# Relu and row sum of a 64 MB input: 8-row tiles, a tail in places of its own, and the last row in halves

## The chip, the cores and the metric

The kernel runs on one core of a Trainium2 chip. The metric is the device time of one execution in microseconds (us); the profile's span, from the first to the last instruction, is about 2 us shorter. SyncE issues the DMAs here; ACT is ScalarE and DVE is VectorE. A DMA moves its bytes over 16 DMA engines in packets, each of which is one record of the trace.

## The reference

```python
x = np.random.randn(32, 512, 1024).astype(np.float32)   # 64 MiB
out = np.sum(np.maximum(x, 0), axis=-1)                  # (32, 512), float32
```

The input is read once, each element gets one max and one add, and 64 KB are written.

## The kernel before

The 16,384 rows are laid over 128 partitions, 128 rows each, so a partition's rows lie one after another in HBM. A tile takes T = 4 rows of each partition: 128 runs of 16 KB, 2 MB. SyncE issues the loads into four buffers; ACT sums two rows of a tile and DVE the other two, each row with one instruction that also accumulates. The last four rows come as tiles of 2, 1 and 1.

```python
    T = 4
    NBIG = R // T - 1
    NBUF = 4
    specs = [(i * T, T, [0, 1], [2, 3]) for i in range(NBIG)]
    r = NBIG * T
    specs.append((r, 2, [1], [0]))
    specs.append((r + 2, 1, [], [0]))
    specs.append((r + 3, 1, [], [0]))
    # ... cut
            for t, (r0, nr, act_rows, dve_rows) in enumerate(specs):    # SyncE
                b = t % NBUF
                if act_cnt[b] > 0:
                    sync.wait_ge(act_sems[b], act_cnt[b])
                if dve_cnt[b] > 0:
                    sync.wait_ge(dve_sems[b], dve_cnt[b])
                sync.dma_start(
                    bufs[:, b, : nr * D],
                    xv[:, r0 : r0 + nr, :],
                ).then_inc(dma_sems[b], 16)
    # ... cut
                    ins = dve.tensor_scalar(          # DVE, one row
                        tile, tile, 0.0, None, MAX, ADD,
                        accum_out=sums[:, g : g + 1],
                    )
```

## Time and profile before

| | before |
|---|---|
| time, median of 3 runs | 166.65 us (166.57 to 166.73) |
| span of the profiled run | 164.4 us |
| DVE / ACT busy | 47% / 43% |
| DMA in mid-stream, 80 to 120 us | 430 GB/s |
| last load landed, output issued | 161.04 us, 162.37 us |

First the page's row of DMA activity: the span in 40 slices, a digit being the mean busy share of the 16 DMA engines in tenths, and below it what they moved.

```profile
DMA  5999999999999999999999999999999999999980
GB/s 191 427 383 431 439 435 419 431 439 431 423 427 439 419 401 435 425 427 431 439 415 431 435 431 427 423 443 423 419 435 431 427 423 443 423 419 435 409 363 18
DMA packets 5042, 67.19 MB, mean 409 GB/s; under 512 B 560, under 2 KB 688, under 8 KB 944
```

The DMA engines are busy from the second slice to the last but two. Nothing can be gained in mid-stream by issuing loads sooner; only a cheaper way to move the same bytes counts.

The view of SyncE's waits (who waited for whom: total us, times, longest) looks alarming and is not:

```profile
SPq L70 <- DVE bufs L121: 139.3, 30, 7.7
```

SyncE waits for a free buffer nearly all the time, but two or three loads are always queued behind the one that runs: in the median a load lands 17.1 us after its issue, and the loads land 4.9 us apart. The queue's own waiting is the normal state of a kernel bound by transfers.

The chain of waits (start, duration, what) shows the pace in mid-stream and the end:

```profile
107.08 2.38 DVE bufs L121 x4
...
126.68 2.38 DVE bufs L121 x4
...
146.26 2.38 DVE bufs L121 x4
...
148.71 11.11 DMA bufs<-in_x_dram
...
159.83 1.23 DVE bufs L121 x2
...
161.06 1.22 DVE bufs L121
```

DVE starts a tile as soon as it has landed, so its starts are landings: 19.58 to 19.60 us for four tiles of 4 rows, which is 9.79 us for 8 rows. At the end the last row lands at 161.04, and DVE then takes 1.22 us for its 1024 columns before the sums can be stored. The timeline (start, duration, engine, line, operation) has both:

```profile
161.06 1.22 DVE L121 TENSOR_SCALAR_CACHE_REDUCE bufs<-bufs 128x1024 f32<-128x1024 f32 x1
...
162.37 0.34 SPq L85 DMA_DIRECT2D out_dram<-sums  x1
```

### The profile page before, as it was taken

To read this page: it belongs to the slowest core of one execution; us is meant where nothing else is said; L and a number is where in the kernel's file an instruction comes from. 1 tells how busy PE (TensorE), PEld (TensorE's weight loads), DVE (VectorE), ACT (ScalarE), POOL (GpSimd) and SP (SyncE) were. 2 spreads that over 40 slices of the span, in tenths; PEclk is the share of its full clock that TensorE was granted. 3 is DMA by queue.
4 is the path that set the end of the run, shared out by engine and by line. 5 is a ranking of instruction groups with operands and counts; after the bars stand their busy time and mean duration, and the time that the engine had idled before them with its cause. 6 is when DMAs were issued, how large, how long until landed. Compare 5 with 4: busy or idle time off the path is not lost.

```text
span 164.4 us, 354 instructions
## 1 busy us (share of the span) xinstructions
DVE 77.1 (47%) x130; ACT 70.3 (43%) x127; POOL 0.2 (0%) x4
## 2 busy tenths in 40 slices
DVE  0055433555433455433455533455533455543394
ACT  3055433455433455433455533455533355543370
POOL 0000000000000000000000000000000000000000
DMA  5999999999999999999999999999999999999980
GB/s 191 427 383 431 439 435 419 431 439 431 423 427 439 419 401 435 425 427 431 439 415 431 435 431 427 423 443 423 419 435 431 427 423 443 423 419 435 409 363 18
DMA packets 5042, 67.19 MB, mean 409 GB/s; under 512 B 560, under 2 KB 688, under 8 KB 944
## 3 DMA queue, kind: packets, MB, share of 16 engines
q1 hardware_dynamic: 5040, 67.18, 96.7%
q14 instruction: 2, 0.02, 0.0%
HBM read 67.11 MB, written 0.07 MB: 409 GB/s over the span
## 4 chain that ended last, share of the span: by engine, by line
DMA 85%; DVE 13%; issue 0%; SPq 0%; DVEq 0%
DMA bufs<-in_x_dram 85%; DVE bufs L121 13%; SPq L70 0%; DVEq L53 0%
## 5 line engine op out<-in xcount | busy, mean ns | idle before, releaser
L121 DVE TENSOR_SCALAR_CACHE_REDUCE bufs<-bufs 128x1024 f32<-128x1024 f32 x65 | 76.8, 1217 | 85.2 <-DMA bufs<-in_x_dram 85.1
L100 ACT ACTIVATE bufs<-bufs 128x1024 f32<-128x1024 f32 x63 | 66.0, 1048 | 88.7 <-DMA bufs<-in_x_dram 88.7
L100 ACT ACTIVATION_READ_ACCUMULATOR bufs<-bufs 128x1 f32 x63 | 11.7, 186 | 0.0
L121 DVE DVE_READ_ACCUMULATOR bufs<-bufs 128x1 f32 x65 | 5.4, 83 | 0.0
L100 ACT ACT_TABLE_LOAD x1 | 1.3, 1283 | 0.7 <-PEq L145 0.7
L145 POOL MEMSET const-bfloat16-1.0<- 128x1 bf16 x1 | 0.1, 101 | 0.0
L145 POOL MEMSET const-uint8-127<- 128x1 uint8 x1 | 0.1, 101 | 0.0
L145 POOL MEMSET const-float32-0.0<- 128x1 f32 x1 | 0.1, 98 | 0.2 <-issue 0.2
L145 POOL MEMSET const-float32-1.0<- 128x1 f32 x1 | 0.1, 98 | 0.0
## 6 DMA issues: line engine op xcount, KB each, us to landing
bufs<-in_x_dram SPq DMA_DIRECT2D x31, 2048.0 KB, 17.1
bufs<-in_x_dram SPq DMA_DIRECT2D x1, 1024.0 KB, 14.7
bufs<-in_x_dram SPq DMA_DIRECT2D x2, 512.0 KB, 9.3
out_dram<-sums SPq DMA_DIRECT2D x1, 64.0 KB, 1.5
```

Source lines behind the costliest of these rows:

```text
L100: ins = act.activation(tile, tile, RELU, accum_out=sums[:, g : g + 1],)
L121: ins = dve.tensor_scalar(tile, tile, 0.0, None, MAX, ADD, accum_out=sums[:, g : g + 1],)
L145: nc = _bacc.Bacc("TRN2", target_bir_lowering=False, num_devices=1)
```

## The change

It means to keep more bytes in flight with fewer DMAs, to issue the last loads without waiting, and to shorten what is left to compute when the last bytes have landed. Tiles have 8 rows (4 MB, runs of 32 KB), in three buffers. The last 8 rows come as tiles of 4, 2 and 1 rows and two halves of a row, each in a place of its own, so nothing holds back their issue. DVE sums the two halves of the last row into two columns and adds them; a wait on a semaphore stands ahead of the add.

```diff
-    T = 4
-    NBIG = R // T - 1
-    NBUF = 4
+    T = 8
+    NBUF = 3
+    H = D // 2
     ... (cut: items of 8 rows, half of them to ACT, half to DVE)
+    items.append(dict(rows=(r, 4), act=[(0, D, r), (D, D, r + 1)],
+                      dve=[(2 * D, D, r + 2), (3 * D, D, r + 3)]))
+    items.append(dict(rows=(r + 4, 2), act=[(D, D, r + 5)], dve=[(0, D, r + 4)]))
+    items.append(dict(rows=(r + 6, 1), act=[(0, D, r + 6)], dve=[]))
+    items.append(dict(half=(r + 7, 0), act=[], dve=[(0, H, r + 7)], notrack=True))
+    items.append(dict(half=(r + 7, H), act=[], dve=[(0, H, "scratch")], dve_post_add=r + 7))
+    # the last items have a place of their own: they are issued without a wait
+    OWN = [-5, -4, -3, -2, -1]
     ... (cut: buffers and semaphores for them)
+                if post is not None:
+                    dve.wait_ge(half_sem, 2)
+                    dve.tensor_tensor(
+                        sums[:, post : post + 1],
+                        sums[:, post : post + 1],
+                        scratch[:, 0:1],
+                        ADD,
+                    ).then_inc(dve_sems[b], 1)
```

More of the change, by code (lines that the diff above doesn't have):

```diff
@@ L1 @@
+from contextlib import ExitStack
 import concourse.bass as bass
@@ L28, in bass_relu_sum_kernel @@
     ADD = mybir.AluOpType.add
-    specs = [(i * T, T, [0, 1], [2, 3]) for i in range(NBIG)]
-    r = NBIG * T
-    specs.append((r, 2, [1], [0]))
-    specs.append((r + 2, 1, [], [0]))
-    specs.append((r + 3, 1, [], [0]))
-    assert sum(s[1] for s in specs) == R
+    items = []
+    nbig = (R - T) // T
+    for i in range(nbig):
+        r0 = i * T
+        act = [(j * D, D, r0 + j) for j in range(T // 2)]
+        dve = [(j * D, D, r0 + j) for j in range(T // 2, T)]
+        items.append(dict(rows=(r0, T), act=act, dve=dve))
+    r = nbig * T
+    assert R - r == T == 8
+    items.append(
+        dict(
+            rows=(r, 4),
+            act=[(0, D, r), (D, D, r + 1)],
+            dve=[(2 * D, D, r + 2), (3 * D, D, r + 3)],
+        )
+    )
+    items.append(
+        dict(rows=(r + 4, 2), act=[(D, D, r + 5)], dve=[(0, D, r + 4)])
+    )
+    items.append(dict(rows=(r + 6, 1), act=[(0, D, r + 6)], dve=[]))
+    items.append(
+        dict(half=(r + 7, 0), act=[], dve=[(0, H, r + 7)], notrack=True)
+    )
+    items.append(
+        dict(
+            half=(r + 7, H),
+            act=[],
+            dve=[(0, H, "scratch")],
+            dve_post_add=r + 7,
+        )
+    )
+    OWN = [-5, -4, -3, -2, -1]
+    own_cols = []
+    own_width = 0
+    for k, i in enumerate(OWN):
+        n = items[i]["rows"][1] * D if "rows" in items[i] else H
+        own_cols.append((own_width, n))
+        own_width += n
+        items[i]["slot"] = NBUF + k
     with (
+        ExitStack() as stack,
         nc.sbuf_tensor([P, NBUF, T * D], F) as bufs,
+        nc.sbuf_tensor([P, own_width], F) as tail,
         nc.sbuf_tensor([P, R], F) as sums,
+        nc.sbuf_tensor([P, 2], F) as scratch,
         nc.semaphore() as dma_sem0,
@@ L42, in bass_relu_sum_kernel @@
         nc.semaphore() as dma_sem2,
-        nc.semaphore() as dma_sem3,
         nc.semaphore() as act_sem0,
@@ L46, in bass_relu_sum_kernel @@
         nc.semaphore() as act_sem2,
-        nc.semaphore() as act_sem3,
         nc.semaphore() as dve_sem0,
@@ L50, in bass_relu_sum_kernel @@
         nc.semaphore() as dve_sem2,
-        nc.semaphore() as dve_sem3,
+        nc.semaphore() as half_sem,
         nc.semaphore() as out_sem,
@@ L54, in bass_relu_sum_kernel, with slot, target_ap @@
     ):
-        dma_sems = [dma_sem0, dma_sem1, dma_sem2, dma_sem3]
-        act_sems = [act_sem0, act_sem1, act_sem2, act_sem3]
-        dve_sems = [dve_sem0, dve_sem1, dve_sem2, dve_sem3]
+        dma_sems = [dma_sem0, dma_sem1, dma_sem2]
+        act_sems = [act_sem0, act_sem1, act_sem2]
+        dve_sems = [dve_sem0, dve_sem1, dve_sem2]
+        for k in range(len(OWN)):
+            dma_sems.append(stack.enter_context(nc.semaphore(f"dma_own{k}")))
+            act_sems.append(stack.enter_context(nc.semaphore(f"act_own{k}")))
+            dve_sems.append(stack.enter_context(nc.semaphore(f"dve_own{k}")))
+        def slot(b):
+            if b < NBUF:
+                return bufs[:, b, :]
+            c0, n = own_cols[b - NBUF]
+            return tail[:, c0 : c0 + n]
+        def target_ap(tgt):
+            if tgt == "scratch":
+                return scratch[:, 0:1]
+            return sums[:, tgt : tgt + 1]
         @block.sync
         def _(sync):
-            act_cnt = [0] * NBUF
-            dve_cnt = [0] * NBUF
+            act_cnt = [0] * (NBUF + len(OWN))
+            dve_cnt = [0] * (NBUF + len(OWN))
             act_last = None
             dve_last = None
-            for t, (r0, nr, act_rows, dve_rows) in enumerate(specs):
-                b = t % NBUF
+            for t, it in enumerate(items):
+                b = it.get("slot", t % NBUF)
                 if act_cnt[b] > 0:
@@ L70, in _ @@
                     sync.wait_ge(dve_sems[b], dve_cnt[b])
-                sync.dma_start(
-                    bufs[:, b, : nr * D],
-                    xv[:, r0 : r0 + nr, :],
-                ).then_inc(dma_sems[b], 16)
-                if act_rows:
+                if "rows" in it:
+                    r0, nr = it["rows"]
+                    sync.dma_start(
+                        slot(b)[:, : nr * D],
+                        xv[:, r0 : r0 + nr, :],
+                    ).then_inc(dma_sems[b], 16)
+                else:
+                    rr, c0 = it["half"]
+                    sync.dma_start(
+                        slot(b)[:, :H],
+                        xv[:, rr, c0 : c0 + H],
+                    ).then_inc(dma_sems[b], 16)
+                if it["act"]:
                     act_cnt[b] += 1
                     act_last = (b, act_cnt[b])
-                if dve_rows:
+                if it["dve"] and not it.get("notrack"):
                     dve_cnt[b] += 1
@@ L89, in _ @@
         def _(act):
-            dcnt = [0] * NBUF
-            for t, (r0, nr, act_rows, dve_rows) in enumerate(specs):
-                b = t % NBUF
+            dcnt = [0] * (NBUF + len(OWN))
+            for t, it in enumerate(items):
+                b = it.get("slot", t % NBUF)
                 dcnt[b] += 1
-                if not act_rows:
+                works = it["act"]
+                if not works:
                     continue
                 act.wait_ge(dma_sems[b], 16 * dcnt[b])
-                for i, rr in enumerate(act_rows):
-                    g = r0 + rr
-                    tile = bufs[:, b, rr * D : (rr + 1) * D]
-                    ins = act.activation(
-                        tile,
-                        tile,
-                        RELU,
-                        accum_out=sums[:, g : g + 1],
-                    )
-                    if i == len(act_rows) - 1:
+                for i, (off, n, tgt) in enumerate(works):
+                    tile = slot(b)[:, off : off + n]
+                    ins = act.activation(tile, tile, RELU, accum_out=target_ap(tgt))
+                    if i == len(works) - 1:
                         ins.then_inc(act_sems[b], 1)
@@ L110, in _ @@
         def _(dve):
-            dcnt = [0] * NBUF
-            for t, (r0, nr, act_rows, dve_rows) in enumerate(specs):
-                b = t % NBUF
+            dcnt = [0] * (NBUF + len(OWN))
+            for t, it in enumerate(items):
+                b = it.get("slot", t % NBUF)
                 dcnt[b] += 1
-                if not dve_rows:
+                works = it["dve"]
+                if not works:
                     continue
                 dve.wait_ge(dma_sems[b], 16 * dcnt[b])
-                for i, rr in enumerate(dve_rows):
-                    g = r0 + rr
-                    tile = bufs[:, b, rr * D : (rr + 1) * D]
+                post = it.get("dve_post_add")
+                for i, (off, n, tgt) in enumerate(works):
+                    tile = slot(b)[:, off : off + n]
                     ins = dve.tensor_scalar(
@@ L127, in _ @@
                         ADD,
-                        accum_out=sums[:, g : g + 1],
+                        accum_out=target_ap(tgt),
                     )
-                    if i == len(dve_rows) - 1:
-                        ins.then_inc(dve_sems[b], 1)
+                    if i == len(works) - 1:
+                        if it.get("notrack") or post is not None:
+                            ins.then_inc(half_sem, 1)
+                        else:
+                            ins.then_inc(dve_sems[b], 1)
+                if post is not None:
[6 more added lines that the diff above has]
+                    ).then_inc(dve_sems[b], 1)
 _INS = ['x']
```

## The prediction

> **What bounds the kernel now.** Loading the input. The page's DMA row reads 9 (90% or more) in 38 of 40 slices; the windows view gives a DMA share of 0.99 to 1.03 and 422 to 434 GB/s nearly everywhere from 16 to 154 us. DVE is busy 47%, ACT 43%; in the waits view both wait only for the loads. SyncE's waits on DVE (139 us) cost nothing: the queue stays about three 2 MB tiles deep. So deeper and wait-free placement of tiles has no wait to remove. What is left is the cost per packet, the start and the tail.
>
> **Per packet.** In the trace's DMA records a 16 KB packet takes 612 ns (median), 8 KB 313, 4 KB 161, and each engine adds a 9 ns semaphore packet per DMA: 36.5 to 37 ns per KB and 10 to 14 ns fixed. Landings agree: 2 MB tiles land 4.89 us apart, the 1 MB one 2.49 us after its predecessor, the 512 KB one 1.27 us: 0.05 to 0.09 us fixed per DMA. Eight-row tiles make one 32 KB run per partition where there were two of 16 KB. If that is one packet, I estimate 1.21 us for it, so each pair of old tiles saves 8 x (10 to 14) + 9, about 0.1 us. Fifteen pairs: about 1.5 us. The new tail has one DMA more and 2 KB packets: minus 0.1. Net 1.4 us, all on the critical path. If the run is split into 16 KB packets, only 0.1 us remains. The Trainium skill (DMA: Bandwidth & Descriptors, section Bandwidth) gives a port ceiling of 435 GB/s; the trace is already near 428, so about 1.5% is the most to be had here.
>
> **Start.** Unchanged: first issue at 0.73 us, bytes near 2 us. The first tile lands later (about 12.8 instead of 8.15 us), at no cost: 4 rows on DVE are about 4.7 us per 9.7 us tile. The slow packets of the first 10 us (up to 1.6 us each) stay.
>
> **Tail.** In the chain of waits the last tile lands at 161.04 us; then DVE takes 1.22 us for 1024 columns, and the output DMA 1.5 us. After, the last piece is 512 columns: 1.22 less 512 columns at 1.04 ns (estimate) is 0.69 us; then a wait and a one-column add, about 0.16 us by the Trainium skill's add formula (VectorE: DVE Perf Modes, section The TRN2 errata; no run here shows it yet) plus some 0.05 for the semaphore. Together 0.9: 0.3 us saved.
>
> **Sum.** 166.65 - 1.4 - 0.3 = 164.95 with 32 KB packets, about 166.2 if split (one chance in five): 165.1 us, range 164.4 to 166.2. Faster by over 2%: 0.02; within 2%: 0.97; slower by over 2%: 0.01.
>
> **What would show it.** About 3,020 packets instead of 5,042, of about 1.21 us each for 32 KB; tiles landing 9.70 us apart instead of 9.79 per two; about 431 GB/s in mid-stream instead of 427; DMA row still all nines; SyncE's waits large and harmless; last landing to output issue about 0.9 instead of 1.3 us.
>
> **What would make it wrong.** The 32 KB runs are split; 32 KB packets are slower per byte; an engine that lags the other fifteen (the last of 16 landings comes 0.3 us after the fifteenth already) lags more; DVE is still busy with the first half when the last lands; longer setup or teardown with twice the semaphores, outside the span (166.65 against 164.4).

## The result, and the profile after

The changed kernel took 164.83 us (median of 12 runs, 164.37 to 165.24), the kernel before 166.65 (15 runs, 166.37 to 167.98). The ratio is 0.9882, with a 95% interval of 0.9863 to 0.9901. A ratio here is the mean time of one kernel's fast runs over that of the other's of the same rounds, so not quite the ratio of the medians. The difference of 1.8 us is clear of the scatter.

The DMA row and packets after:

```profile
DMA  5999999999999999999999999999999999999990
GB/s 201 433 433 393 449 425 433 433 433 441 425 377 465 409 425 449 405 449 425 417 449 433 417 457 417 433 441 409 449 433 417 457 425 409 457 417 405 407 366 26
DMA packets 3026, 67.19 MB, mean 411 GB/s; under 512 B 336, under 2 KB 464, under 8 KB 848
```

From the second slice on the row is nines nearly to the end, as before. The packets fell from 5042 to 3026: a 32 KB run is one packet. (The prediction worked this out as about 3,020.)

SyncE's waits, where the longest one doubled at no cost, since a tile now takes twice as long to load:

```profile
SPq L124 <- DVE bufs L179: 119.6, 12, 16.1
```

The chain of waits:

```profile
92.17 4.66 DVE bufs L179 x8
...
121.31 4.66 DVE bufs L179 x8
...
127.83 31.90 DMA tail<-in_x_dram
...
159.75 1.33 DVE tail L179 x4
...
161.11 0.16 DVE sums L195
```

The two DVE starts are three tiles of 8 rows apart: 29.14 us, or 9.71 us per 8 rows, against 9.79 before. That is the gain in the stream. The first half of the last row was issued at 127.83 us and landed 31.9 us later, most of it spent in the queue: early issue buys a place in a queue, not an earlier landing.

The last instructions, from the timeline (start, duration, engine, line, operation; in brackets the idle time before it):

```profile
159.75 0.69 DVE L179 TENSOR_SCALAR_CACHE_REDUCE tail<-tail 128x512 f32<-128x512 f32 x1 [0.68 <-DMA tail<-in_x_dram]
...
160.38 0.69 DVE L179 TENSOR_SCALAR_CACHE_REDUCE tail<-tail 128x512 f32<-128x512 f32 x1
160.99 0.08 DVE L179 DVE_READ_ACCUMULATOR tail<-tail 128x1 f32 x1
161.11 0.16 DVE L195 TENSOR_TENSOR sums<-sums,scratch 128x1 f32<-128x1 f32 x1
161.34 0.35 SPq L147 DMA_DIRECT2D out_dram<-sums  x1
```

The second half landed at 160.36 by the trace's landing records, and DVE began it at 160.38: it had just finished with the first half. From last landing to the issue of the output it is 0.98 us, where it was 1.33 (161.04 to 162.37). The one-column add takes 0.158 us on the page, which is what the Trainium skill's add formula gives for one column (VectorE: DVE Perf Modes, section The TRN2 errata: 152 cycles at 0.96 GHz).

### The profile page after: what moved, and what is told of

It is laid out like the page before. It is cut to its first block, busy times and chain, and to the rows that moved or that the text cites. A ratio compares the mean times of both kernels' runs of the same rounds, so it can differ in the third digit from the quotient of the medians.

```text
span 163.3 us, 325 instructions
## 1 busy us (share of the span) xinstructions
DVE 74.8 (46%) x131; ACT 69.8 (43%) x129; POOL 0.2 (0%) x4
## 2 busy tenths in 40 slices
DMA packets 3026, 67.19 MB, mean 411 GB/s; under 512 B 336, under 2 KB 464, under 8 KB 848
## 4 chain that ended last, share of the span: by engine, by line
DMA 84%; DVE 12%; SPq 2%; issue 0%
DMA bufs<-in_x_dram 65%; DMA tail<-in_x_dram 20%; DVE bufs L179 11%; SPq L127 1%; DVE tail L179 1%; DVE sums L195 0%; SPq L124 0%
## 5 line engine op out<-in xcount | busy, mean ns | idle before, releaser
L179 DVE TENSOR_SCALAR_CACHE_REDUCE bufs<-bufs 128x1024 f32<-128x1024 f32 x60 | 69.6, 1216 | 85.4 <-DMA bufs<-in_x_dram 85.4
L162 ACT ACTIVATE bufs<-bufs 128x1024 f32<-128x1024 f32 x60 | 62.6, 1044 | 88.7 <-DMA bufs<-in_x_dram 88.7
L162 ACT ACTIVATION_READ_ACCUMULATOR bufs<-bufs 128x1 f32 x60 | 11.2, 187 | 0.0
L179 DVE TENSOR_SCALAR_CACHE_REDUCE tail<-tail 128x1024 f32<-128x1024 f32 (+1 forms) x5 | 4.9, 1005 | 1.0 <-DMA tail<-in_x_dram 0.9
L162 ACT ACTIVATE tail<-tail 128x1024 f32<-128x1024 f32 x4 | 4.2, 1053 | 1.0 <-DMA tail<-in_x_dram 0.9
L162 ACT ACTIVATION_READ_ACCUMULATOR tail<-tail 128x1 f32 x4 | 0.7, 187 | 0.0
```

Of the source, the lines that this page charges most:

```text
L162: ins = act.activation(tile, tile, RELU, accum_out=target_ap(tgt))
L179: ins = dve.tensor_scalar(tile, tile, 0.0, None, MAX, ADD, accum_out=target_ap(tgt),)
```

## The experiments

The theory: most of the gain is a fixed time per DMA packet, paid half as often with 32 KB packets; the rest is the shorter last piece of work. Rivals: the deeper queue and the wait-free tail give the gain; or the cost belongs to each DMA rather than to each packet; or the split of the last row is worth nothing. All twelve runs gave correct results. The diffs are cut to the lines that matter (semaphores made in a loop and the count of big tiles are left out).

### 1. Two DMAs per 8-row tile

```diff
-                    sync.dma_start(slot(b)[:, : nr * D], xv[:, r0 : r0 + nr, :]).then_inc(dma_sems[b], 16)
+                    parts = 2 if nr == T else 1
+                    m = nr // parts
+                    for p in range(parts):
+                        sync.dma_start(
+                            slot(b)[:, p * m * D : (p + 1) * m * D],
+                            xv[:, r0 + p * m : r0 + (p + 1) * m, :],
+                        ).then_inc(dma_sems[b], 16)
-                dcnt[b] += 1
+                dcnt[b] += 2 if b < NBUF else 1
```

> The changed kernel, with each 8-row tile loaded by two DMAs of 4 rows on the same semaphore: the same buffers, waits, queue depth and tail, but 16 KB packets as before. Packet theory (the gain is mainly the fixed time of each packet): about 1.45 us slower than the changed kernel's 164.83, that is 166.3, with about 5,100 packets. Rival (deeper queue and wait-free tail placement give the gain): stays at 164.8.

Measured: 165.88 us (165.63 to 166.31), the kernel before on that chip 166.33; ratio 0.9967 (0.9941 to 0.9994). The page counts 5186 packets. The changed kernel itself was not in this call; the nearest to it there is the kernel of experiment 4, which has the 32 KB packets but the last row whole, and took 164.71 us. This one is 1.17 us slower than that, although buffers, waits and depth are the same and its tail is the better one (by 0.21 us, experiment 8): together 1.4, where 1.45 was expected. By ratio, too, most of the gain is gone (0.9967 against the changed kernel's 0.9882 and, later, 0.9921 on other chips).

### 2. One DMA per 8-row tile, but 16 KB packets

```diff
-        nc.sbuf_tensor([P, NBUF, T * D], F) as bufs,
+        nc.sbuf_tensor([P, NBUF, 2, 4 * D + 16], F) as bufs,
     ... (cut)
+                        src = xv[:, r0 : r0 + nr, :].rearrange("p (h q) d -> p h (q d)", h=2)
+                        dst = bufs[:, b, :, : 4 * D]
     ... (cut: the row slices of ACT and DVE skip the gap)
```

> The changed kernel with one DMA per 8-row tile, but a gap of 64 bytes in the buffer after the fourth row, so that a packet can be 16 KB at most. Packet theory: 120 DMAs' worth of semaphore packets fewer than with two DMAs per tile (15 x 9 ns per engine = 0.14 us), otherwise the same: about 166.15, with about 4,900 packets. If the fixed cost belonged to the DMA and not to the packet: 164.8.

Measured on the same chip: 165.23 us (165.04 to 165.32), ratio 0.9924 (0.9902 to 0.9946). The page confirms the packets:

```profile
DMA packets 4947, 67.19 MB, mean 411 GB/s; under 512 B 337, under 2 KB 465, under 8 KB 849
```

(Where the record speaks of 120 DMAs fewer, 15 is meant, as the bracket after it computes.) It is 0.65 us faster than with two DMAs per tile, where 0.14 was expected. That was a miss. Against experiment 4 it is 0.52 us slower, or 0.7 with the tail's 0.21: so the time, too, charges more than half of the gain to packets alone. What decides is the pace of each stream, which does not depend on the scatter at its start: see the table after experiment 7. There the split is 0.057 us per 8 rows for packets and 0.018 for DMAs, so over 15 tiles 0.86 and 0.27. The rest of the 0.65 between this kernel and the two-DMA one, about 0.4, is not explained by either; the profiled run of the two-DMA kernel had more slow packets (18.6 us in all beyond the median, against 13.3, over 16 engines: 0.33 us per engine if evenly spread, which would cover most of it in this one pair of traces).

### 3. Only a deeper queue

The kernel before with eight buffers of 4 rows instead of four.

```diff
-    NBUF = 4
+    NBUF = 8
```

> The kernel before with 8 buffers of 4 rows instead of 4: more bytes in the queue (16 MB instead of 8), the last loads issued some 20 us earlier, nothing else. Packet theory: no change, 166.6 (within 0.2). Rival (depth and removed waits give the gain): about 165.2.

Measured on the same chip: 166.13 us (165.92 to 166.76), ratio 0.9987 (0.9961 to 1.0013). Twice the bytes in flight and loads issued that much earlier change nothing that can be told from the scatter. The interval alone leaves room for up to 0.6 us; the pace in the table below (9.789 us, as without the depth) leaves none in the stream. The rival falls.

### 4. The last row whole

```diff
-    items.append(dict(half=(r + 7, 0), act=[], dve=[(0, H, r + 7)], notrack=True))
-    items.append(dict(half=(r + 7, H), act=[], dve=[(0, H, "scratch")], dve_post_add=r + 7))
+    items.append(dict(rows=(r + 7, 1), act=[], dve=[(0, D, r + 7)]))
-    OWN = [-5, -4, -3, -2, -1]
+    OWN = [-4, -3, -2, -1]
```

> The changed kernel with the last row loaded and summed whole (no halves, no add). Tail theory: from last landing to the output's issue 1.33 us again instead of 0.98, one small DMA less (0.1 us back): about 0.25 to 0.3 us slower than the changed kernel, 165.1. Rival (the split tail is worth nothing, or costs): 164.8 or less.

Measured on the same chip: 164.71 us (164.65 to 165.02), ratio 0.9896 (0.9874 to 0.9918). Against the changed kernel on another chip this says nothing about 0.25 us. It was run again in experiment 8.

### 5. Everything but the 8-row tiles

```diff
-    T = 8
-    NBUF = 3
+    T = 4
+    NBUF = 6
```

> The changed kernel with 4-row tiles (6 buffers, the same 96 KB a partition), own places and split tail kept: everything of the change but the tile size. Packet theory: 30 tiles x (8 x 612 + 9 ns) against 15 x (8 x 1213 + 9): 1.45 us slower than the changed kernel, 166.3. Rival: 164.8.

Measured on a second chip, where the kernel before took 165.73 us (165.57 to 165.85): 165.43 us (165.24 to 165.50), ratio 0.998 (0.9968 to 0.9993). Own places, no waits in the tail, six buffers and the split last row together are worth 0.3 us. (166.3 was expected; experiment 8 shows by how much that was too high.)

### 6. 2-row tiles

```diff
-    T = 8
-    NBUF = 3
+    T = 2
+    NBUF = 12
```

> The changed kernel with 2-row tiles (12 buffers, the same 96 KB): 8 KB packets. Packet theory: 60 x (8 x 313 + 9) against 15 x (8 x 1213 + 9) ns: 5.1 us slower than the changed kernel, 169.9. A rival that sees the gain in depth or in the tail: 164.8 to 166.

Measured on the same chip: 167.46 us (167.43 to 167.54), ratio 1.0106 (1.0091 to 1.0121). The direction is right: the dose that makes it worse works. The size is not: it is 2.0 us slower than with 4-row tiles, where the sums gave 3.65 (5.1 less 1.45); the pace in the table below gives 0.16 us per 8 rows, 2.4 us over 15 times 8 rows. The windows view (us, then busy time of DVE, ACT and POOL, clock, DMA share, GB/s) shows the slower stream in a stretch without disturbance, for the kernel before, the changed kernel and this one:

```profile
80.00:120.00 40.00, 19.01 (x34) 17.51 (x32) 0.00 (x0) 1.00 1.01 430
```

```profile
80.00:120.00 40.00, 18.59 (x32) 17.07 (x32) 0.00 (x0) 1.00 1.00 433
```

```profile
80.00:120.00 40.00, 19.64 (x32) 18.39 (x32) 0.00 (x0) 1.00 1.01 422
```

The last column falls from 433 GB/s with 32 KB packets to 430 with 16 KB and 422 with 8 KB, at a DMA share of 1.00 to 1.01 each time: the engines are equally "busy", but part of that is not data. The view can be off by 1 or 2 GB/s, since packets cross the edges of a window; the pace below gives 432, 428.5 and 422.

### 7. 12-row tiles, with the tail as it was and with a longer one

```diff
-    T = 8
+    T = 12
-    nbig = (R - T) // T
+    nbig = (R - 8) // T          # first kernel: 3 buffers, 10 big tiles, tail of 8 rows
+    nbig = (R - 20) // T         # second kernel: 2 buffers, 9 big tiles, then 8, 4, 4, 2, 1, half, half
```

> The changed kernel with ten 12-row tiles and the same 8-row tail: 48 KB packets, estimated 1814 ns. Packet theory: the stream ends 0.5 us sooner, but DVE needs 6 x 1.15 = 6.9 us for its share of the last big tile while the next 4 rows land 4.9 us after it, so DVE runs behind the loads in the tail and issues the output about 1.1 us later than the loads would allow: in sum about 165.4. If the drain didn't matter: 164.3.

> Nine 12-row tiles (2 buffers) and a longer tail of 8, 4, 4, 2, 1 and two half rows, all in places of their own, so that each piece is computed while the next lands: 48 KB packets without the drain. Packet theory: 0.4 us faster than the changed kernel, 164.4. If two buffers are too few, the DMA row would show gaps and the time would be above 164.8.

Measured on the chip of 5 and 6: 165.10 us (165.00 to 165.32), ratio 0.9965, with the tail as it was, and 164.19 us (164.09 to 164.25), ratio 0.9907, with the longer tail (165.4 and 164.4 were expected). The end of the first one's timeline:

```profile
156.28 1.21 DVE L170 TENSOR_SCALAR_CACHE_REDUCE tail<-tail 128x1024 f32<-128x1024 f32 x1
...
159.70 0.68 DVE L170 TENSOR_SCALAR_CACHE_REDUCE tail<-tail 128x512 f32<-128x512 f32 x1
...
160.31 0.68 DVE L170 TENSOR_SCALAR_CACHE_REDUCE tail<-tail 128x512 f32<-128x512 f32 x1
...
161.27 0.35 SPq L138 DMA_DIRECT2D out_dram<-sums  x1
```

There is no idle time in brackets: DVE no longer waits for loads. The last half row had landed at 159.36 by the trace, and DVE reached it at 160.31, 0.95 us later, because it still had six rows of the last big tile to do. Its output is issued 1.91 us after the last landing, against 0.98 for the changed kernel. The tail has to shrink in steps that DVE can follow; with the longer tail the 0.9 us are not lost.

The pace of the stream, worked out for all kernels from the trace's landing records: for each tile the median of its 16 landings (one per DMA engine), taken from row 72 to row 96, a stretch with hardly any slow packets, and divided by three. The last column is the number of traces. In experiment 1 two DMAs share a semaphore, but the landings of one end at least 3.7 us before those of the next begin, so they can be told apart.

| packets | per 8 rows and engine: packets, DMAs | us per 8 rows | traces |
|---|---|---|---|
| 48 KB | 5.3, 0.67 | 9.689 to 9.692 | 3 |
| 32 KB | 8, 1 | 9.712 to 9.714 | 4 |
| 16 KB, one DMA per 8 rows | 16, 1 | 9.770 | 1 |
| 16 KB, two DMAs per 8 rows | 16, 2 | 9.785 to 9.789 | 5 |
| 8 KB | 32, 4 | 9.946 | 1 |

The same bytes take longer the more packets carry them. From the second and third rows a packet costs 0.057 / 8 = 7 ns; from the third and fourth a DMA costs about 18 ns per engine (one trace against five); from the fourth and fifth, with that taken off for two more DMAs, (0.158 - 0.036) / 16 = 7.6 ns per packet; the first two rows give 6 ns. The packet theory holds, with a DMA's own cost beside it, and depth does not appear: the fourth row holds the kernel before, its deeper version (experiment 3), the 4-row versions of the changed kernel and the two-DMA kernel alike. (What the 64-byte gap of experiment 2 does by itself was not tested; the two-DMA kernel, which has none, is slower still.)

### 8. The changed kernel and three variants on one chip

The same files as in the first comparison and in experiments 4, 5 and 7 (longer tail).

> The changed kernel itself again, on the same chip as the three that follow, because the kernel before differed between chips (166.65, 166.33, 165.73) by as much as the effects to be told apart. From the spacing of tiles in the traces so far (8 rows: 9.785 us in 16 KB packets, 9.713 in 32 KB) 15 tiles save 1.1 us; the tail saves 0.35 less 0.1 for its extra DMA: 1.35 us faster than the kernel before on this chip. If the 1.8 of the first comparison is right: 1.8.

> The last row whole, on the same chip as the changed kernel. Tail theory: 0.25 us slower than the changed kernel. Rival (the split is worth nothing, as the first comparison across chips seemed to say): the same within 0.1.

> Everything of the change but the 8-row tiles, on the same chip as the changed kernel. Packet theory with the spacing measured: 1.1 us slower than the changed kernel, and 0.25 faster than the kernel before. Rival: as fast as the changed kernel.

> Nine 12-row tiles and the longer tail, on the same chip as the changed kernel. 8 rows in 48 KB packets were 9.687 us apart, against 9.713: over 108 rows 0.35 us, less about 0.05 for one more DMA: 0.3 us faster than the changed kernel. If larger packets are worth nothing beyond 32 KB: the same.

| kernel | median us (range) | against the changed kernel | ratio to before |
|---|---|---|---|
| before | 165.79 (165.66 to 165.89) | +1.31 | 1 |
| changed | 164.48 (164.34 to 164.62) | 0 | 0.9921 |
| last row whole | 164.69 (164.60 to 164.79) | +0.21 | 0.9933 |
| 4-row tiles | 165.44 (165.39 to 165.48) | +0.96 | 0.9979 |
| 12-row tiles, longer tail | 164.36 (164.10 to 164.62) | -0.12 | 0.9915 |

The change is worth 1.31 us here, where 1.35 was expected. The tile size is 0.96 of it (1.1 expected) and the split of the last row 0.21 (0.25 expected). The 0.14 that remain are not told from zero with medians of five to nine runs. The ends of the two timelines behind the 0.21 (changed, then last row whole):

```profile
159.57 0.69 DVE L179 TENSOR_SCALAR_CACHE_REDUCE tail<-tail 128x512 f32<-128x512 f32 x1
...
160.53 0.35 SPq L147 DMA_DIRECT2D out_dram<-sums  x1
```

```profile
159.61 1.22 DVE L169 TENSOR_SCALAR_CACHE_REDUCE tail<-tail 128x1024 f32<-128x1024 f32 x1 [1.27 <-DMA tail<-in_x_dram]
...
160.91 0.35 SPq L137 DMA_DIRECT2D out_dram<-sums  x1
```

In both the last piece starts at about 159.6 us; with the half row the output is issued 0.38 us sooner. Comparing the median engine from row 96 on, the split tail's one more DMA takes 0.06 us back (158.92 - 119.81 against 158.83 - 119.78).

12-row tiles keep their faster pace (9.692 us) but cannot be told from the changed kernel in time, where 0.3 us was expected. The trace of that run has 74 packets more than 3% over their median, 17.1 us in all, starting from 2 to 70 us, where the changed kernel's trace has 18 of them, 11.3 us. Whether that is chance or goes with 48 KB packets is open: the other 12-row traces had 21 and 23.

## Why the prediction was right or wrong

The time, 164.83 us, is inside the range and 0.3 from the forecast of 165.1.

- *The kernel is bound by the load, and the change has no wait to remove.* Right. The DMA row was nines nearly throughout in both (37 slices before, not 38 as the prediction says), and eight buffers alone gave a ratio of 0.9987 with 1 inside its interval.
- *32 KB runs are single packets.* Right: 3026 packets, and the trace has them at a median of 1213 ns (estimate 1.21 us).
- *The fixed cost of packets saves 1.5 us, less 0.1 for the tail's DMA.* The mechanism was right and the term too large. The pace went from 9.79 to 9.71 us per 8 rows (forecast: 9.79 to 9.70), so the difference is 0.075 us per tile and not 0.1: 1.1 us over 15 tiles, and 0.96 on one chip in time. The mistake lay in adding the durations of packets. The line through 612, 313 and 161 ns has 10 to 14 ns fixed, but a packet costs the stream about 7 ns: the records of neighbouring packets must overlap by some ns, for 16 packets of 612 ns and two of 9 sum to 9.81 us where the stream took 9.79, and in the run with 2-row tiles 32 of 312 ns and four of 9 to 10.02 where it took 9.95. The forecast for 2-row tiles (5.1 us slower than the changed kernel, by the sums) showed it more plainly. The spacing of landings was the better source, and it was in the trace already: the prediction read 0.05 to 0.09 us from it.
- *The tail saves 0.3 us.* Right: 0.35 us from last landing to output (1.33 to 0.98), and 0.21 in time with its own DMA taken off. The half row took 0.69 us and the add 0.158, as estimated.
- *The start is unchanged.* Roughly. In experiment 8 the median engine had landed row 24 at 32.27 us with 8-row and at 32.18 with 4-row tiles, although at its own pace the former should be 0.2 us ahead. Slow packets account for that in these two traces: up to row 24, those more than 3% over the median took 10.3 us beyond it with 8-row tiles and 3.6 us with 4-row tiles, 0.4 us more per engine if evenly spread. Whether larger packets bring it about is not shown: up to row 24 the traces with 32 KB packets have 10.3 to 11.1 us, but those with 16 KB anything from 3.6 to 16.6.
- *Setup outside the span does not grow.* Right: time less span is 1.9 us in the profiled runs of both (166.33 - 164.4, 165.17 - 163.3).

The sum of the terms on the prediction's own path (with 32 KB packets) was 1.7 us. The first comparison gave 1.8, but the one on a chip with less scatter gave 1.31, which is about what pace and tail add up to (1.1 and 0.35, less 0.06 for the tail's DMA). So the close agreement with 1.8 is partly luck. Where the other half microsecond came from in the first comparison is not settled: its runs scattered by 1.6 us for the kernel before, and the profiled runs of the two kernels are 1.16 us apart (166.33 and 165.17). Slow packets are a candidate. In the traces with 16 KB packets and more they took 4.7 to 24.5 us in all over 16 engines, that is 0.3 to 1.5 us per engine if evenly spread, and landings follow them: the time at which the median engine has landed row 96, less twelve times the pace, is 2.7 to 3.8 us in the 14 traces, and with the slow packets up to then taken off (over 16) it is 2.2 to 2.6 us. But which of the runs without a trace had many is not known.

## What to carry to other kernels

Where the DMA engines were busy all the time, as here, deeper buffers and earlier issue bought nothing; look then at what a byte costs, and make the contiguous run of each packet longer until the fixed part is small, which here was worth 0.6%. Larger tiles want a tail that shrinks in steps, so that the compute of each piece fits into the loading of the next: with 12-row tiles and the old tail 0.9 us was lost there. To judge effects of 0.2 to 1 us, put the kernels on one chip, and read the pace from landings rather than from sums of packet times.

## What the Trainium skill lacked or had wrong

- DMA: Bandwidth & Descriptors, section Bandwidth, asks for at least 1 MiB per DMA to reach 75% of peak and lists 341 GB/s for 1 MB. In a queued stream of 1 MiB DMAs (2-row tiles) the run here held 422 GB/s; the cost of a further DMA was about 18 ns per engine. The page's figure is for DMAs issued from GpSimd, these were issued from SyncE; the section should say that transfers queued behind each other hide most of the fixed time of one (a stream of 1 MiB loads stands on this page only in another section, on iDMA).
- The same section (Why small descriptors are slow) has a fixed cost of about 3 cycles per packet and speaks of descriptors of a few hundred bytes. It gives no figure for large ones. Here a packet costs the stream about 7 ns at 8 to 32 KB, and going from 16 to 32 KB runs, with half as many DMAs, was worth 0.96 us of 165. The ceiling of 435 GB/s was not reached: 433 in mid-stream with 32 KB packets.
- No page was found that tells of slow packets: in the kernel before 41 of 3968 16 KB packets took over 3% longer than the median, up to 1621 ns against 612, 28 of them in the first 10 us. Nor does one give a size for the spread between engines: the slowest of 16 engines landed the last tile 0.6 to 1.0 us after the median one in all 14 traces.
- VectorE: DVE Perf Modes, section The TRN2 errata, has an add formula that it checks at 512 and 2048 columns; it held at one column too: 0.158 us.
